# A two-layer diffusion backbone on one Trainium2 core: a third score bank, fill matmuls ordered against the scores, and modulation steps moved to other stages

## The chip, the core and the metric

The kernel runs on one NeuronCore of a Trainium2 chip, in float32 throughout. A core has five engines with instruction queues of their own: TensorE (PE in the profile, its weight loads PEld), VectorE (DVE), ScalarE (ACT), GpSimd (POOL) and SyncE (SP, which here only issues DMAs). Matmuls write to PSUM, which this program divides into 8 banks of 128 x 512 float32; all other tiles lie in SBUF. The metric is the device time of one execution in microseconds (us), the median of several runs.

## The reference

Two layers work on 1024 latent tokens (a 16 x 64 grid) and 256 context tokens, all of width 1024. In each layer every token is normalized and modulated by a shift, a scale and a gate, which come from a product of a condition vector with a 1024 x 3072 matrix (the "modulation"; the latents have one condition, the context another). Layer 0 is grouped attention (a global half A and a windowed half B), layer 1 a convolution module beside neighbourhood attention.

```python
for i in range(2):
    sh_l, sc_l, g_l = split3(silu(c)     @ mod_w[i] + mod_b[i])
    sh_c, sc_c, g_c = split3(silu(c_ctx) @ mod_w[i] + mod_b[i])
    h_lat = rms_norm(x_lat, norm_g[i]) * (1 + sc_l) + sh_l
    h_ctx = rms_norm(x_ctx, norm_g[i]) * (1 + sc_c) + sh_c
    if i == 0:
        y_lat, y_ctx = even_mixer(h_lat, h_ctx, ...)
    else:
        y_lat, _ = odd_mixer(h_lat, h_ctx, ...)     # the context is not updated
    x_lat = x_lat + g_l * y_lat
    if i == 0: x_ctx = x_ctx + g_c * y_ctx
return rms_norm(x_lat, final_g)

# even_mixer: q, k, v, gate = h @ w_in, 16 query heads on 4 key heads
#   A: RMS-normed q and k, rotary, softmax over all 1280 keys
#   B: rotary, softmax over 256 context keys and a band of +-128, with a sink logit
#   y = concat(o * silu(gate)) @ w_out
# odd_mixer: 31-tap depthwise convolution + LayerNorm on 512 channels,
#   and 8 heads that each see 8 x 16 neighbours and the context, with a bias table
```

The last layer's context is not updated, so of layer 1's gate only the latents' side is needed.

## The kernel before

The order of the work is not written out instruction by instruction. The program traces its operations in order, gives each a priority, and a planner (with a cost model of its own) then puts the instructions of each engine into one fixed order and assigns buffers. `later(n)` adds `n` to the priority number of what is traced in it, so that it gives way to other work that is ready. `tc.issue_after(x)` orders TensorE instructions of a block behind the instruction `x` on TensorE's own queue; it adds no wait on the chip beyond that order.

**Three-term products.** Each float32 operand is split into a high part (a cast on ScalarE) and a low part (a subtraction, mostly on GpSimd), `split` at L294. A product is then three matmuls, `mm3` (L317): high x high, high x low, low x high.

**Layer 0.** The four key heads are four units `u`, taken in the order 2, 3 (half B, 42 score tiles each) and 0, 1 (half A, 84 tiles each). I call them the first to the fourth pair. The stages are:

- Startup: x is loaded, shift and scale of layer 0 are computed by `mod_half` and `mod_half_v`, and h is made.
- Solo (`solo[0]` is true): `fill0(0)` (L865, L872) projects q, k, v of the first pair and half of its gate, with no attention beside it.
- Three stages of the loop at L883. `weave` (L495) steps the attention generator `attn_gen` (L392) `nmain` times and deals `nfill` steps of a second generator between: `proj_qkv` and `proj_gate` of the next pair. `NSTEP` holds a unit's steps (two a tile), `NLAST` (L50) how many of them lie beside the gate, `NFILL` (34 each) the steps of the projection of q, k and v. Fill is traced with `later(80)` (`FL`).
- The fourth pair's attention runs beside `out0_part` (L1009), the output projection of the finished pairs; `O1` (L71) deals attention steps to its four pieces. Then come the last output projection and the norm of layer 1 (L1055 to L1096).

A tile in `attn_gen` is: a score of two matmuls (L465, L469; for masked tiles one more), an exponential on ScalarE (L477, `pf`), the split into `ph` and `pl` (L479), and, three tiles later (`LOOK0`), three matmuls into the sum `ov` (L409 to L411). Before a group of 512 queries starts, `attn_prep` (L364) computes row maxima through `mx` banks (L576, L588, L596), transposes them (`trn`, L387) and writes them into QL.

**PSUM.** `BUFS` (L97) deals the 8 banks: `pp` 2 (projections), `mx` 2 (maxima), `st` 2 (scores), `ov` 1, `tr` 1. The `tr` bank holds the transposes of projected q and k (`trk`, L836), those of the maxima, the sums of modulation (`trm`, L223) and the sums of squares (`trs`, L248). In solo stages `pp` requests go round over `pp` and `mx`.

**Modulation.** `mod_steps` (L849) yields eight halves (two of layer 0's gate, then six of layer 1's shift, scale and gate, 512 columns each). A half is eight rows of weights, each one step: a load of the row (L202 or L211, on SP), and for each condition one multiply-add on VectorE (L214, L219). Outside the solo stage the second condition's rows 1, 3 and 6 go to ScalarE and GpSimd instead (L216, L217). A ninth step sums over partitions with TensorE. `tick` (L739) is called three times in each block of 24 projection matmuls and takes a modulation step at every call in the solo stage and at every third otherwise (`TICK0, TICK1`).

**Layer 1.** Four convolution projections with the convolution beside them, then `d_proj(0)` and `d_proj(1)` (L1167), the second with the LayerNorm steps of L1125 beside it, then the attention with `d_proj(2)`, `d_proj(3)` and the output projection woven in.

Of the kernel before, what the change touches and what calls it, by code (L numbers as in the profile page):

```python
# [49 lines left out]
NLAST = (48, 28)  # L50
# [18 lines left out]
NFILL = (34, 34, 34)  # L69
HV = (('gggvvvvg',) * 3, ('gggvvvvg', 'vvvgvvvg', 'gggvvvvg'))  # L70
O1 = (6, 84, 46, 14)  # L71
TICK0, TICK1 = (1, 3)
# [15 lines left out]
def tile_kernel(ctx: ExitStack, tc: tile.TileContext, a, out):  # L88
# [8 lines left out]
    BUFS = {"pp": 2, "mx": 2, "st": 2, "ov": 1, "tr": 1}  # L97
# [3 lines left out]
    sts, pvs = [], []  # L101

# [66 lines left out]
    def mod_half(pool, l, part, j):  # L169
# [11 lines left out]
        tr = bank("tr", nm("trm"))  # L181
# [11 lines left out]
    def mod_half_v(pool, l, part, j, conds):  # L193
# [28 lines left out]
        for n_, (q, t) in enumerate(zip(conds, accs)):  # L222
            tr = bank("ov" if solo[0] else "tr", nm("trm"))  # L223
# [20 lines left out]
    def rstd_steps(pool, accs, n, tag, inv=1.0, tr="tr"):  # L244
# [70 lines left out]
    done = [None]  # L315
# [48 lines left out]
    def attn_prep(pool, g):  # L364
# [21 lines left out]
        tr2 = bank("tr", nm("trn"))  # L386
# [5 lines left out]
    def attn_gen(pool, groups, vshare, look, nexts=None):  # L392
# [57 lines left out]
        for x, (g, t) in enumerate(items):  # L450
# [14 lines left out]
            sts.append(PE.matmul(st[:, :n], KA[:, cs], g.QH[:, q0 : q0 + n], start=True, stop=False))  # L465
# [29 lines left out]
    def weave(main, nmain, fill, nfill, last=True, all_fill=True, lag=0):  # L495

        done = 0
        for k in range(nmain):
            next(main, None)
            while done * nmain < (k + 1) * nfill:  # L500
                with ExitStack() as cx:
                    cx.enter_context(later(FL[layer[0]]))
                    if lag and len(sts) >= lag:
                        cx.enter_context(tc.issue_after(sts[-lag].ins))
                    next(fill, None)
                done += 1
# [145 lines left out]
    with ExitStack() as p0x:  # L652
# [6 lines left out]
        with tc.tile_pool(name="st0", bufs=1, reuse_waits="tile") as st0:  # L659
# [31 lines left out]
            def norm_bc(c, acc):  # L691
                n = CHUNKS[c][1]
                return run(rstd_steps(st0, [acc], n, "st"))[:, :n]
# [45 lines left out]
        def tick():  # L739
            beat[0] += 1  # L740
            if beat[0] % (TICK0 if solo[0] else TICK1) == 0:
# [25 lines left out]
        def proj_gate(u, ms):  # L767
# [4 lines left out]
            for m, c in ms:  # L772
                t0, n = CHUNKS[c]
                pp = bank("pp", nm("pg"))
                for dk in range(DK):
# [3 lines left out]
                    if dk % 3 == 1:  # L779
                        tick()  # L780
# [8 lines left out]
        def proj_qkv(u, w):  # L789
            wh, wl = w or load_w0("ev_qkv", u, 384)  # L790
            for jp in range(5):
                pc = ap.tile([P, 2, 384], F32, tag="pc", name=nm("pc"), bufs=PCB)
                for jj in range(2):
                    j = 2 * jp + jj
                    pp = bank("pp", nm("pq"))
                    for dk in range(DK):
                        mm3(pp[:, :384], Hs(h, 0, j * P, P, dk), Hs(h, 1, j * P, P, dk), wh[dk], wl[dk],
                            dk == 0, dk == DK - 1)
                        if dk % 3 == 1:
                            tick()  # L800
# [33 lines left out]
        def qk_tail(u, j, pc):  # L834

            tr = bank("tr", nm("trk"))  # L836
# [12 lines left out]
        def mod_steps():  # L849
# [3 lines left out]
            for part in range(3):  # L853
                for j in range(2):
                    yield from mod_half_v(ap, 1, part, j, (0, 1) if part < 2 else (0,))
# [27 lines left out]
        for k in range(3):  # L883
            u = ORDER[k]
            n = NSTEP[u // 2] + (12 if k == 0 else 0)
# [3 lines left out]
            weave(main, n - n0 - NLAST[u // 2], fill0(k + 1), NFILL[k], False)  # L889
            weave(main, NLAST[u // 2], proj_gate(ORDER[k + 1], gblocks(k + 1)[1]), 18, False)  # L890
# [79 lines left out]
    with tc.tile_pool(name="o0", bufs=1, reuse_waits="tile", side="right") as op_:  # L970
# [93 lines left out]
        weave(main, O1[1], out0_part(parts[0]), 48, False)  # L1064
        weave(main, O1[2], chain(load_oh(parts[1]), out0_part(parts[1])), 30, False)
# [568 lines left out]
```

## Time and profile before

| | us |
|---|---|
| median of 3 runs | 1557.82 |
| lowest and highest run | 1554.83, 1560.38 |
| the profiled execution | 1555.72 |
| its span (first to last instruction) | 1553.9 |
| mean granted TensorE clock | 0.967 of full speed |

Times in rows of the profile count from the span's start. "Busy" is the time in which an engine ran at least one instruction. A row of a group ends with the idle time of its engine just before its instructions and what ended most of it. The granted clock of a stretch is the mean share of full speed that TensorE had.

### The profile page before, as it was taken

The page shows a single profiled execution, that of the slowest core. Times are in us where ns is not written, and L with a number is a line of the kernel's source. Part 1 is how long each engine was busy: PE and PEld are TensorE (multiplying, and loading weights), DVE is VectorE, ACT ScalarE, POOL GpSimd, SP SyncE. Part 2 cuts the span into 40 slices and gives each one's busy share as a digit, 9 for nine tenths or more (in the row PEclk, how much of TensorE's full clock was granted, in tenths as well). Part 3 has the DMA queues.
Part 4 walks back from the last instruction along what each step waited for, and adds up shares of the span by engine and source line. Part 5 has one row for each costly group of instructions (what it writes and reads, how often), then busy time and mean ns, then how long its engine had stood idle before and what let it go on. Part 6 is the DMA issues. An engine that isn't in the chain of part 4 may idle for free.

```text
span 1553.9 us, 22052 instructions
## 1 busy us (share of the span) xinstructions
PE 1449.1 (93%) x6984; PEld 1172.3 (75%) x6984; DVE 1123.3 (72%) x2172; ACT 759.8 (49%) x1545; POOL 833.5 (54%) x762
## 2 busy tenths in 40 slices
PE   6989989999999989899999889999999999799995
PEld 1878868887789678678887668888787787687784
DVE  4998898689858666654577677999755457586776
ACT  2721354445454755565455555443434455545563
POOL 1561464555555676675455666664542443545574
PEclk9999999999999999999999999999999999899996
DMA  9548245423441124631111121213456888788623
GB/s 339 194 146 270 79 125 174 147 64 121 151 129 44 54 89 143 207 115 56 42 45 35 68 95 57 80 63 123 158 178 222 272 225 263 221 264 240 192 92 109
DMA packets 185614, 221.01 MB, mean 142 GB/s; under 512 B 17421, under 2 KB 139481, under 8 KB 185497
## 3 DMA queue, kind: packets, MB, share of 16 engines
q1 hardware_dynamic: 178832, 208.03, 43.1%
q10 hardware_dynamic: 6664, 11.57, 2.3%
q8 instruction: 55, 0.90, 0.2%
q14 instruction: 63, 0.51, 0.1%
HBM read 159.51 MB, written 60.03 MB: 141 GB/s over the span
## 4 chain that ended last, share of the span: by engine, by line
PE 67%; DVE 12%; DMA 11%; issue 3%; POOL 3%; ACT 2%; SPq 2%; DVEq 0%; ACTq 0%; POOLq 0%
PE p L320 6%; PE p L318 6%; PE p L319 6%; PE ov L409 4%; PE ov L410 4%; PE ov L411 4%; PE st L465 4%; PE po L318 4%; PE st L469 4%; PE po L319 4%; PE po L320 4%; PE pq L320 2%; PE pq L319 2%; PE pq L318 2%; DMA mw<-in_mod_w_dram 2%
## 5 line engine op out<-in xcount | busy, mean ns | idle before, releaser
L299 POOL TENSOR_TENSOR pl<-pf,ph 128x512 fp32r<-128x512 f32 (+4 forms) x321 | 399.9, 1258 | 270.7 <-ACT ph L296 218.9
L299 POOL TENSOR_TENSOR wl<-wr,wh 128x256 fp32r<-128x256 f32 (+2 forms) x256 | 197.7, 788 | 227.9 <-ACT wh L296 203.3
L477 ACT ACTIVATE pf<-st 128x512 f32<-128x512 f32 x284 | 166.2, 596 | 161.7 <-PE st L469 106.3
L296 ACT CAST ph<-pf 128x512 fp32r<-128x512 f32 (+4 forms) x364 | 209.2, 588 | 25.5 <-PE ov L410 17.6
L296 ACT CAST wh<-wr 128x256 fp32r<-128x256 f32 (+2 forms) x264 | 103.2, 404 | 172.2 <-DMA wr<-in_od_d_dram 39.3
L318 PE MATMUL p<-hh,wh 128*128 128x512 f32 x448 | 177.7, 399 | 3.7 <-DVE spk L299 1.4
L319 PE MATMUL p<-hl,wh 128*128 128x512 f32 x448 | 177.9, 398 | 0.2 <-POOL hl L299 0.2
L320 PE MATMUL p<-hh,wl 128*128 128x512 f32 x448 | 175.2, 399 | 0.1
L465 PE MATMUL st<-QH,KAt 128*128 128x512 f32 (+4 forms) x364 | 144.0, 397 | 19.8 <-ACT pf L477 16.5
L409 PE MATMUL ov<-ph,Vt 128*128 128x512 f32 (+4 forms) x364 | 143.6, 394 | 8.8 <-DVE y L631 6.4
L411 PE MATMUL ov<-pl,Vt 128*128 128x512 f32 (+4 forms) x364 | 143.7, 395 | 3.9 <-POOL pl L299 3.8
L410 PE MATMUL ov<-ph,Vt 128*64 128x512 f32 (+4 forms) x364 | 140.8, 387 | 0.0
L469 PE MATMUL st<-QL,KBt 68*128 68x512 f32 (+4 forms) x364 | 138.2, 388 | 0.8 <-DVE QL L388 0.7
L1116 DVE SCALAR_TENSOR_TENSOR cps<-U,taps,cps 128x512 f32<-128x512 f32 x184 | 124.3, 747 | 0.0
L589 DVE TENSOR_REDUCE mp<-mx 128x1 f32<-128x512 f32 x128 | 85.5, 682 | 33.5 <-PE mx L588 32.7
L219 DVE SCALAR_TENSOR_TENSOR macc<-mw,csil,macc 128x512 f32<-128x512 f32 x107 | 97.5, 929 | 14.0 <-DMA mw<-in_mod_w_dram 13.2
L318 PEld LDWEIGHTS p<-hh,wh 128*128 128x128 f32 x448 | 84.6, 189 | 24.5 <-DVE spk L299 1.6
L465 PEld LDWEIGHTS st<-QH,KAt 128*128 128x128 f32 x364 | 69.8, 192 | 42.5 <-ACT pf L477 25.3
L319 PEld LDWEIGHTS p<-hl,wh 128*128 128x128 f32 x448 | 84.6, 189 | 20.4 <-POOL hl L299 0.6
L320 PEld LDWEIGHTS p<-hh,wl 128*128 128x128 f32 x448 | 84.6, 189 | 20.3 <-POOL wl L299 1.0
L411 PEld LDWEIGHTS ov<-pl,Vt 128*128 128x128 f32 x364 | 71.1, 195 | 28.1 <-POOL pl L299 7.6
L409 PEld LDWEIGHTS ov<-ph,Vt 128*128 128x128 f32 x364 | 71.5, 196 | 24.3 <-issue 7.0
(277 smaller groups left out, 3518.4 us busy)
## 6 DMA issues: line engine op xcount, KB each, us to landing
mw<-in_mod_w_dram SPq DMA_DIRECT2D x34, 512.0 KB, 5.6
bs<-in_d_bs_dram SPq DMA_DIRECT2D x16, 832.0 KB, 7.3
Q<-qs SPq DMA_DIRECT2D x40, 256.0 KB, 2.7
QH<-Q SPq DMA_DIRECT2D x80, 128.0 KB, 2.7
bm<-in_d_bm_dram SPq DMA_DIRECT2D x16, 540.0 KB, 6.1
wr<-in_od_d_dram SPq DMA_DIRECT2D x64, 128.0 KB, 2.6
mw<-in_mod_w_dram SPq DMA_DIRECT2D x28, 256.0 KB, 3.1
wr<-in_ev_qkv_dram SPq DMA_DIRECT2D x32, 192.0 KB, 3.8
```

The lines of the kernel that those rows point to most:

```text
L296: SC.copy(hi, src)
L299: (GP if leng == "g" else VE).tensor_tensor(lo, src, hi.bitcast(F32), op=ALU.subtract)
L318: PE.matmul(o, lh, rh, start=first, stop=False)
L319: PE.matmul(o, lh, rl, start=False, stop=False)
L320: done[0] = PE.matmul(o, ll, rh, start=False, stop=last)
L409: PE.matmul(o, V[:, 64:192], ph[:, :n], start=(t == 0), stop=False)
L410: PE.matmul(g.ov[0:64, q0 : q0 + n], V[:, 0:64], ph[:, :n], start=False, stop=False)
L411: pvs.append(PE.matmul(o, V[:, 64:192], pl[:, :n], start=False, stop=(last and g.sink is None)))
L465: sts.append(PE.matmul(st[:, :n], KA[:, cs], g.QH[:, q0 : q0 + n], start=True, stop=False))
L469: PE.matmul(st[:, :n], KB[0:68, cs], g.QL[0:68, q0 : q0 + n], start=False, stop=True)
L477: SC.activation(pf[:, :n], st[:, :n], AF.Exp, scale=1.0 if g.bias else SCALE)
L1116: VE.scalar_tensor_tensor(pc, uc, w, pc, op0=ALU.mult, op1=ALU.add)
```

## The change

- PSUM: `st` gets three banks, `tr` is gone. Its users move: transposed maxima and modulation sums to `mx`, transposed q and k to `TRV`, which is `pp`, sums of squares in startup and LayerNorm to `st`.
- Attention steps: `NLAST` now goes by stage, 28, 28, 56. The third stage ends 36 steps earlier (`SHIFT`), and these steps run at the start of the next one, where `O1` becomes 6, 110, 66.
- Fill: in the first two stages of the loop a fill step may not be ordered ahead of the score eight back (`LOOSE`). In the third and in the output projections it may not be ahead of the score four back (`HOLD`), and a score may not be ahead of the last fill matmul two fill steps back (`TIE`). The third stage's first eight fill steps are traced ahead of it (`NPRE`).
- Modulation: a step at every second tick in the solo stage, at every second beside a gate and at every third beside the projection of pairs 2 and 3; none beside that of pairs 0 and 1, which also normalize q and k. Layer 1's gate leaves `mod_steps` and becomes `mod_gate1`, stepped beside `d_proj(1)`.

```diff
-NLAST = (48, 28)
+NLAST = (28, 28, 56)
+HOLD, TIE, LOOSE = 4, 2, 8
+NPRE = (0, 0, 8)
-O1 = (6, 84, 46, 14)
-TICK0, TICK1 = (1, 3)
+O1 = (6, 110, 66, 14)
+SHIFT = 36
+TICKS, TICKQ, TICKG = (2, 3, 2)
...
-    BUFS = {"pp": 2, "mx": 2, "st": 2, "ov": 1, "tr": 1}
+    BUFS = {"pp": 2, "mx": 2, "st": 3, "ov": 1}
+    tied = [None]
...
-        tr = bank("tr", nm("trm"))
+        tr = bank("st", nm("trm"))
...
-            tr = bank("ov" if solo[0] else "tr", nm("trm"))
+            tr = bank("ov" if solo[0] else "mx", nm("trm"))
...
-        tr2 = bank("tr", nm("trn"))
+        tr2 = bank("mx", nm("trn"))
...
-    done = [None]
+    done = prods = [None]
...
-            sts.append(PE.matmul(st[:, :n], KA[:, cs], g.QH[:, q0 : q0 + n], start=True, stop=False))
+            with ExitStack() as cx:
+                if tied[0] is not None:
+                    cx.enter_context(tc.issue_after(tied[0].ins))
+                sts.append(PE.matmul(st[:, :n], KA[:, cs], g.QH[:, q0 : q0 + n], start=True, stop=False))
...
-    def weave(main, nmain, fill, nfill, last=True, all_fill=True, lag=0):
+    def weave(main, nmain, fill, nfill, last=True, all_fill=True, lag=0, tie=0):
         done = 0
+        past = []
         for k in range(nmain):
+            tied[0] = past[-tie] if tie and len(past) >= tie else None
             next(main, None)
+            tied[0] = None
             while done * nmain < (k + 1) * nfill:
...
                     next(fill, None)
+                past.append(prods[0])
                 done += 1
...
-        def tick():
+        def tick(every):
             beat[0] += 1
-            if beat[0] % (TICK0 if solo[0] else TICK1) == 0:
+            if beat[0] % (TICKS if solo[0] else every) == 0:
...
-                        tick()
+                        tick(TICKG)
...
-                            tick()
+                            if u > 1:
+                                tick(TICKQ)
...
-            tr = bank("tr", nm("trk"))
+            tr = bank(TRV, nm("trk"))
...
-            for part in range(3):
+            for part in range(2):
                 for j in range(2):
-                    yield from mod_half_v(ap, 1, part, j, (0, 1) if part < 2 else (0,))
+                    yield from mod_half_v(ap, 1, part, j, (0, 1))
...
-            n = NSTEP[u // 2] + (12 if k == 0 else 0)
+            n = NSTEP[u // 2] + (12, 0, -SHIFT)[k]
...
-            weave(main, n - n0 - NLAST[u // 2], fill0(k + 1), NFILL[k], False)
-            weave(main, NLAST[u // 2], proj_gate(ORDER[k + 1], gblocks(k + 1)[1]), 18, False)
+            hold = dict(lag=HOLD, tie=TIE) if k == 2 else dict(lag=LOOSE)
+            fill = fill0(k + 1)
+            for _ in range(NPRE[k]):
+                with later(FL[0]):
+                    next(fill)
+            weave(main, n - n0 - NLAST[k], fill, NFILL[k] - NPRE[k], False, **hold)
+            weave(main, NLAST[k], proj_gate(ORDER[k + 1], gblocks(k + 1)[1]), 18, False, **hold)
...
-        weave(main, O1[1], out0_part(parts[0]), 48, False)
-        weave(main, O1[2], chain(load_oh(parts[1]), out0_part(parts[1])), 30, False)
+        weave(main, O1[1], out0_part(parts[0]), 48, False, lag=HOLD, tie=TIE)
+        weave(main, O1[2], chain(load_oh(parts[1]), out0_part(parts[1])), 30, False, lag=HOLD, tie=TIE)
...
-        nh = [norm_h(0, "st", "tr"), norm_h(1, "pp", "tr"), norm_h(2, "st", "tr")]
-        weave(main, NSTEP[U1 // 2] - O1[0] - O1[1] - O1[2], through_attention(), O1[3])
+        nh = [norm_h(0, "st", "mx"), norm_h(1, "pp", "mx"), norm_h(2, "st", "mx")]
+        weave(main, NSTEP[U1 // 2] + SHIFT - O1[0] - O1[1] - O1[2], through_attention(), O1[3])
...
+    def mod_gate1():
+
+        for j in range(2):
+            c0 = 2048 + j * 512
+            acc = kvp.tile([P, 512], F32, tag="QH", name=nm("macc"), bufs=3)
+            for dk in range(DK):
+                w = kvp.tile([P, 512], F32, tag="QL", name=nm("mw"), bufs=3)
+                SY.dma_start(w, a["mod_w"][1, dk * P : (dk + 1) * P, c0 : c0 + 512])
+                if dk == 0:
+                    VE.tensor_scalar(acc, w, csil[:, dk, 0:1], None, op0=ALU.mult)
+                else:
+                    VE.scalar_tensor_tensor(acc, w, csil[:, dk, 0:1], acc, op0=ALU.mult, op1=ALU.add)
+                yield
+            tr = bank("ov", nm("trm"))
+            for i in range(4):
+                PE.matmul(tr[:, 2 * i : 2 * i + 2], acc[:, i * P : (i + 1) * P], one, start=True, stop=True)
+            o = 16 + j * 4
+            VE.tensor_tensor(modT[1][:, o : o + 4, 0], tr[:, 0:8].rearrange("p (i c) -> p i c", c=2)[:, :, 0],
+                             modb[:, 1, o : o + 4], op=ALU.add)
+            yield
...
-            bc = yield from rstd_steps(vp, [s1], 512, "st", 2.0)
+            bc = yield from rstd_steps(vp, [s1], 512, "st", 2.0, "st")
...
             bg = lns()
+            m1 = mod_gate1()
             for _ in d_proj(1):
                 pump(1)
+                next(m1, None)
             for _ in bg:
                 pass
+            run(m1)
```

More of the change, by code (lines that the diff above doesn't have):

```diff
@@ L242, in newton_rsqrt, with rstd_steps @@
         return r
-    def rstd_steps(pool, accs, n, tag, inv=1.0, tr="tr"):
+    def rstd_steps(pool, accs, n, tag, inv=1.0, tr="mx"):
         nb = n // P
@@ L692, in norm_bc @@
                 n = CHUNKS[c][1]
-                return run(rstd_steps(st0, [acc], n, "st"))[:, :n]
+                return run(rstd_steps(st0, [acc], n, "st", tr="st"))[:, :n]
             made = [0]
```

## The prediction

> **What bounds the kernel now.** I read the page first, then busy time by stage, then who waits inside the stages that the change touches.
>
> ```profile
> span 1553.9 us, 22052 instructions
> PE 1449.1 (93%) x6984; PEld 1172.3 (75%) x6984; DVE 1123.3 (72%) x2172; ACT 759.8 (49%) x1545; POOL 833.5 (54%) x762
> ```
>
> TensorE is busy for 93% of the span, so 104.8 us of it are idle. The same number of matmuls runs after the change, so a gain can only come out of idle or slow TensorE time. The stages (columns: length, then busy us and instructions of PE, PEld, DVE, ACT, POOL, then granted clock, DMA share, GB/s):
>
> ```profile
> 60.00:160.00 100.00, 92.48 (x527) 85.67 (x526) 91.64 (x131) 32.48 (x68) 42.44 (x34) 0.97 0.58 182
> 160.00:290.00 130.00, 123.91 (x632) 103.69 (x632) 103.83 (x228) 59.75 (x139) 68.82 (x57) 0.96 0.42 126
> 290.00:460.00 170.00, 160.40 (x821) 134.28 (x820) 138.01 (x294) 83.89 (x184) 93.86 (x77) 0.99 0.40 121
> 460.00:660.00 200.00, 186.49 (x871) 147.98 (x870) 137.86 (x249) 111.80 (x200) 131.32 (x100) 0.97 0.34 106
> 660.00:880.00 220.00, 219.13 (x1038) 174.84 (x1037) 138.47 (x248) 119.95 (x227) 131.57 (x113) 1.00 0.20 64
> 880.00:920.00 40.00, 29.48 (x128) 22.45 (x127) 28.25 (x49) 24.46 (x53) 26.15 (x27) 0.83 0.07 20
> 1120.00:1210.00 90.00, 87.78 (x430) 71.77 (x429) 42.94 (x83) 33.09 (x72) 32.24 (x35) 1.00 0.63 203
> ```
>
> In order these are the solo stage (first pair's projections beside modulation), the attention of the first, second and third head pair with the next pair's projections as fill, the fourth pair with the output projection, layer 0's end, and layer 1's second pair of projections. Stage 660 to 880 is full: 0.9 us idle at clock 1.00. The five others of layer 0 idle for 7.5, 6.1, 9.6, 13.5 and 10.5 us. Idle time also costs clock:
>
> ```profile
> 404.50:406.50 2.00, 0.06 (x2) 0.08 (x1) 1.93 (x3) 1.89 (x4) 1.88 (x2) 1.00 0.58 171
> 406.50:409.90 3.40, 3.40 (x12) 2.80 (x13) 3.40 (x6) 0.00 (x0) 1.88 (x2) 0.50 0.26 86
> 563.50:570.30 6.80, 6.16 (x15) 4.38 (x15) 2.06 (x5) 3.90 (x8) 4.50 (x7) 0.50 0.27 80
> ```
>
> A pause of 2 us at 404.5 is followed by 3.4 us at half clock, which is 1.7 us more lost. Taken as length times (1 - clock), the five stages lose 3.0, 5.2, 1.7, 6.0 and 6.8 us that way. So 10.5, 11.3, 11.3, 19.5 and 17.3 us are to be had, 69.9 us in all. The Trainium skill, TensorE: Matmul & The Clock Gate, "HAM oscillation — how this bites in real kernels", says that pauses longer than about 3.4 us bring the low clock. By it the 2 us pause would cost only itself, and the low clock would have another cause that stays; the rows show it right behind 2 us, which is shorter. What that would make of the sum is a rival below.
>
> What ends the idle time (waits of TensorE, us in total, times, longest), first for 60 to 160, then 160 to 460, then 460 to 660, then 880 to 920:
>
> ```profile
> PE trk L838 <- DVE qs L299: 6.3, 4, 2.8
> ```
> ```profile
> PE st L465 <- ACT pf L477: 6.3, 8, 2.1
> PE mx L596 <- DVE mp L578: 2.6, 3, 1.4
> PE mx L576 <- DMA QH<-Q: 1.9, 1, 1.9
> ```
> ```profile
> PE st L465 <- ACT pf L477: 7.4, 6, 2.3
> PE mx L576 <- DMA QH<-Q: 2.0, 3, 0.8
> ```
> ```profile
> PE ov L409 <- DVE y L631: 5.1, 1, 5.1
> ```
>
> In the solo stage the one `tr` bank waits for a VectorE that is 92% busy. In the attention stages a score waits for one of two `st` banks, while no fill matmul stands before it in the queue.
>
> **The change, part by part.**
>
> *Modulation moved off the solo stage.* These groups stand in 60 to 160, 160 to 290 and 290 to 450:
>
> ```profile
> L219 DVE SCALAR_TENSOR_TENSOR macc<-mw,csil,macc 128x512 f32<-128x512 f32 x61 | 52.4, 879 | 3.0 <-DMA mw<-in_mod_w_dram 2.3
> L214 DVE TENSOR_SCALAR macc<-mw,csil 128x512 f32<-128x512 f32 x10 | 7.4, 751 | 0.0
> ```
> ```profile
> L219 DVE SCALAR_TENSOR_TENSOR macc<-mw,csil,macc 128x512 f32<-128x512 f32 x18 | 20.3, 1138 | 4.3 <-DMA mw<-in_mod_w_dram 4.2
> ```
> ```profile
> L219 DVE SCALAR_TENSOR_TENSOR macc<-mw,csil,macc 128x512 f32<-128x512 f32 x14 | 14.2, 1015 | 6.8 <-DMA mw<-in_mod_w_dram 6.7
> ```
>
> The solo stage has 39 ticks (30 of the projection, 9 of the gate). Each now gives a step; after, every second does. With the step that completes a loaded pair of weight rows that is 40 steps now, 36 of them rows with two operations each, and 20 after, 18 of them rows. The last step's second operation runs on ScalarE and GpSimd, so VectorE has 71 now (61 + 10 above) and 35 after. 36 operations at 0.88 us leave it: 31.7 us of its 91.6. Then TensorE decides: in back-to-back runs a 384-wide matmul starts every 0.175 us and a 512-wide one every 0.234 us (first and last of each run):
>
> ```profile
> 553.33 0.34 PE L319 MATMUL pq<-wl,hh 128*128 128x384 f32 x1
> 553.86 0.34 PE L319 MATMUL pq<-wl,hh 128*128 128x384 f32 x1
> ```
> ```profile
> 959.68 0.39 PE L318 MATMUL p<-hh,wh 128*128 128x512 f32 x1
> 961.55 0.40 PE L318 MATMUL p<-hh,wh 128*128 128x512 f32 x1
> ```
>
> That puts the stage's TensorE work at 87 us, an estimate: roughly 275 of 384 columns (48), 96 of 512 (22.5), 48 of 256 (5.6), and about 11 for sums and transposes. 13 us are open by this count, 10.5 by the rows; I take **-10**, bounds -20 (the modelled ends of matmuls hide more idle time) and 0.
>
> *The same modulation in attention.* The steps left for it hold 12 two-sided rows and 16 one-sided ones now; after, 30 two-sided rows (the one-sided go to layer 1). With ScalarE and GpSimd doing rows 1, 3 and 6 of the second side, VectorE goes from 36 to 49 operations: 13 more, 14 us at 1.08 us (the mean of the two rows 1138 and 1015), most of it in 160 to 290 (23 of the 34 steps: 4 at the gate left over, 10 beside the plain projection, 9 at its gate). None falls on the projections of the third and fourth pair, where VectorE also normalizes. ScalarE and GpSimd get 12 such operations in place of 5, at 0.72 and 1.28 us each:
>
> ```profile
> L216 ACT ACTIVATE mw<-mw,csil x5: 722/722/727, 158.2 to 242.5; 128x512 f32<-128x512 f32 x5
> L217 POOL TENSOR_TENSOR macc<-macc,mw x5: 1276/1287/1293, 163.4 to 245.1; 128x512 f32<-128x512 f32 x5
> ```
>
> VectorE is 80% busy in 160 to 290, so the 14 us fit into its 26 idle ones only if they come evenly; that is what bounds this term below.
>
> *Third score bank, fill bound loosely (160 to 460).* With three banks a score may start while two wait for ScalarE. Fill may no longer run more than eight scores ahead, so it is there when scores wait. Against it stand the moved steps. Of 22.6 us I take half, **-11**, bounds -22 and +8 (the 14 us, half hidden).
>
> *Where the `tr` bank's users go.* Transposes of q and k share two `pp` banks with the projections. Each holds its bank for a cast and a subtraction, and 40 of them bound the cost at 41 us with no cover:
>
> ```profile
> L296 ACT CAST qs<-trk x40: 460/478/492, 77.3 to 639.4; 128x384 fp32r<-128x384 f32 x40
> L299 DVE TENSOR_TENSOR qs<-trk,qs x40: 510/554/559, 87.3 to 639.9; 128x384 fp32r<-128x384 f32 x40
> ```
> ```profile
> L388 DVE TENSOR_TENSOR QL<-trn,k_bd x56: 681/682/684, 178.2 to 1490.8; 4x512 fp32r<-4x512 f32 x36, 12x512 fp32r<-12x512 f32 x20
> ```
>
> Cover is the attention beside them; without it each costs about 1 us. The transposed maxima share `mx` and hold it 0.68 us, 56 times, 38 us uncovered; they run whole tiles before their scores. Both at 0.
>
> *Third pair: fewer attention steps, fill tied to scores, eight fill steps ahead (460 to 660).* 36 steps, 18 tiles, move on to the fourth pair's stage, so 60 tiles beside 34 fills become 38 beside 26. The move itself is neutral: five matmuls a tile cost the same in either stage. It also pulls the fourth pair's start past this boundary, where output weights and k land:
>
> ```profile
> 640.00:655.00 15.00, 11.92 (x42) 7.58 (x40) 11.90 (x23) 8.20 (x13) 11.33 (x8) 0.89 0.91 287
> ```
> ```profile
> PE po L318 <- ACT wh L296: 1.1, 1, 1.1
> ```
>
> That boundary alone loses 3.1 us idle and 1.6 of clock. Of 19.5 us I take two thirds, **-13**, bounds -19 and 0.
>
> *Fourth pair and layer 0's end.* Output projections spread over 182 of 204 steps in place of 136 of 168, so 14 fills meet the last 22 steps, not 32. The stage is full, so more evenness gives nothing there; a stall of the tie is a rival below. At the end, 5.1 us go by until the group before has been divided and leaves the only `ov` bank, with no fill to run. I take **-4**, bounds -12 and +6.
>
> *Layer 1.* 16 operations of one side come to 1120 to 1210, and 16 loads of 256 KB on SP's queue. Uncontended the operation takes 0.75 us:
>
> ```profile
> L219 DVE SCALAR_TENSOR_TENSOR macc<-mw,csil,macc x107: 734/751/2014, 15.3 to 447.1; 128x512 f32<-128x512 f32 x107
> ```
> ```profile
> L1163 DVE SCALAR_TENSOR_TENSOR uc<-uc,gc 128x512 f32<-128x512 f32 x8 | 5.5, 687 | 9.1 <-DMA gc<-Gc 9.1
> ```
>
> That is 12 us on a VectorE with 47 idle; 4.2 MB at 203 / 0.63 = 322 GB/s is 13 us, with 33 free. But a step that waits for its load holds the LayerNorm behind it, which waits 9.1 us for its own loads and ends just before layer 1's attention can start. I take **+3**, bounds 0 and +12. Layer 1's attention gets the third bank and loses `tr`: **-1**, bounds -4 and +4. The startup uses `st` for sums: 0.
>
> Sum: -10 - 11 - 13 - 4 + 3 - 1 = **-36**. The profiled execution took 1555.72 us (1.8 beside its span), so 1519.7; the median of the runs is 2.1 higher, so **1522**.
>
> **The rivals.**
>
> *VectorE becomes the bound in 160 to 460.* For: 80 to 81% busy, single operations stretched to 1.1 us there, 14 us more. Against: steps go beside gates. The stage's term becomes +4 and half of solo's gain is lost: -16, **1542**.
>
> *The tie stalls attention (slower).* A score now stands behind a fill matmul two fills back in TensorE's queue; when that waits for weights, everything waits. The chain per weight set is load, cast, subtraction:
>
> ```profile
> wr<-in_ev_wo_dram SPq DMA_DIRECT2D x32, 128.0 KB, 2.2
> ```
> ```profile
> L296 ACT CAST wh<-wr 128x256 fp32r<-128x256 f32 (+2 forms) x264 | 103.2, 404 | 172.2 <-DMA wr<-in_od_d_dram 39.3
> L299 POOL TENSOR_TENSOR wl<-wr,wh 128x256 fp32r<-128x256 f32 (+2 forms) x256 | 197.7, 788 | 227.9 <-ACT wh L296 203.3
> ```
>
> That is 3.4 us, with half clock 5.1. Ten sets pass in the tied stages: +51, so +15 net, **1573**; it turns slower from the eighth stalled set. Against: 660 to 880 loads eight of these sets today and idles 0.9 us.
>
> *It does not do what it says.* The planner already places fill so that neither bound binds, and VectorE's work only changes place: solo -10, +7 in attention, +3 in layer 1: about **1558**.
>
> *The low clock does not follow the pauses,* so only idle time can be won: of the terms -38 in layer 0 a share of 22.7 / 69.9, 12 us, falls away: -24, **1534**.
>
> *All of it is recovered:* the longer lookahead and the tie leave no pause to 920: -69.9 + 3 - 1 = -68, **1490**.
>
> **How the numbers follow.** Forecast (1500 to 1545) 0.50; VectorE bound 0.14; tie stalls 0.16; no effect 0.09; clock apart 0.05; all recovered 0.06. The range 1490 to 1573 takes in all of these up to their prices, hence every bound that I hold likely; what it leaves out are several bad ends together. Measurement cannot tell 0.3%, 4.7 us, from no change. Faster: 0.50 + 0.14 + 0.05 + 0.06 = 0.75; same 0.09; slower 0.16.
>
> **What would show it.** Right: the solo stage's VectorE near 60 us and its length near 90; score waits for `pf` well under 13.7 us up to 660; half-clock stretches gone from 160 to 660; clock 1.00 over the third pair; the last wait for `y` shorter. Wrong: TensorE waits of `p`, `po` or `pg` for `wh` or `wl` (tie), `mx` waits for `mp` grown (VectorE), `pq` waits for `qs` or `pc` (shared bank), first `mx` of layer 1 late against the last `uc` (modulation there).

## The result, and the profile after

The changed kernel takes **1641.08 us** (median of 4 runs, 1637.82 to 1642.6) against 1558.13 us for the kernel before (4 runs on the same chip): a ratio of 1.0531, 95% interval [1.0505, 1.0558]. I had forecast 1522 us with a range up to 1573. The direction was wrong, and so was the range. The profiled execution took 1637.82 us, 82.1 more than the one of before.

The page after, total, engines and granted clock:

```profile
span 1635.9 us, 22000 instructions
PE 1489.7 (91%) x6984; PEld 1200.6 (73%) x6984; DVE 1138.8 (70%) x2165; ACT 766.4 (47%) x1552; POOL 842.9 (52%) x769
PEclk9999989899999989999999988999999999899996
```

The same 6984 matmuls run, but TensorE now idles for 146.2 us of the span, not 104.8, and its mean clock fell from 0.967 to 0.941. Where the time lies is read off marks that both traces have, each the first start of a group (us from the span's start):

| mark | before | after | stage longer by |
|---|---|---|---|
| first maximum (attention starts) | 158.9 | 126.4 | -32.5 |
| first maximum of the third pair | 457.6 | 511.2 | +86.1 |
| first output projection of layer 0 | 652.6 | 701.2 | -5.1 |
| first projection of layer 1 | 923.6 | 980.0 | +7.7 |
| first convolution step | 960.5 | 1029.3 | +12.5 |
| first maximum of layer 1 | 1212.7 | 1287.8 | +6.3 |
| end | 1553.9 | 1635.9 | +6.9 |

The first two rows belong together, since the solo stage only handed its work on: +53.6 us by the third pair's first maximum. Layer 1 adds 25.7. The third pair's stage is 5.1 shorter, but fewer matmuls fall in it (see e8). By stage (columns as in the prediction's stage table):

```profile
60.00:125.00 65.00, 58.24 (x328) 53.34 (x327) 58.73 (x80) 27.10 (x58) 38.38 (x29) 0.95 0.44 138
125.00:290.00 165.00, 141.14 (x691) 119.93 (x691) 98.25 (x208) 58.08 (x131) 63.36 (x54) 0.91 0.38 118
290.00:512.00 222.00, 201.52 (x967) 167.66 (x968) 168.21 (x345) 98.16 (x215) 119.05 (x94) 0.94 0.35 104
512.00:702.00 190.00, 175.14 (x805) 140.68 (x804) 129.53 (x229) 104.18 (x189) 121.92 (x92) 0.95 0.31 95
```

From 125 to 512 TensorE idles for 23.9 + 20.5 = 44.4 us, and length times (1 - clock) is 14.9 + 13.3 = 28.2 us: 72.6 together. The two rows of before from 160 to 460 had 15.7 + 6.9 = 22.6. The 50 us between them are nearly all of the 53.6. VectorE is only 60% and 76% busy there, so it isn't short of time. TensorE's waits over the whole span say what is missing:

```profile
PE trn L391 <- DVE nmt L387: 18.6, 8, 5.2
...
PE st L476 <- DVE QL L392: 9.0, 7, 2.6
PE st L472 <- ACT pf L484: 8.4, 12, 3.1
PE mx L587 <- DVE QL L392: 7.9, 9, 2.3
PE pq L322 <- ACT pc L814: 6.8, 2, 4.4
...
PE pq L322 <- DVE sg L344: 4.1, 3, 3.0
```

Score waits for `pf` did fall to 8.4 us; before had

```profile
PE st L465 <- ACT pf L477: 16.5, 17, 2.3
```

What took their place is the end of a group's preparation: `trn` waits for `nmt`, the VectorE result that it transposes, and scores and maxima wait for QL. The eight waits of `trn` shown all lie in 125 to 512. In 160 to 460 of before, `trn` waited twice, for 0.6 and 0.5 us. The third kind of new wait is `pq` for `pc` and `sg`: a projection wants a `pp` bank that another user has not yet emptied.

### The profile page after: what moved, and what is told of

Its sections match the earlier page's. It is cut to its first block, busy times and chain, and to the rows that moved or that the text cites. A ratio compares the mean times of both kernels' runs of the same rounds, so it can differ in the third digit from the quotient of the medians.

```text
span 1635.9 us, 22000 instructions
## 1 busy us (share of the span) xinstructions
PE 1489.7 (91%) x6984; PEld 1200.6 (73%) x6984; DVE 1138.8 (70%) x2165; ACT 766.4 (47%) x1552; POOL 842.9 (52%) x769
## 4 chain that ended last, share of the span: by engine, by line
PE 68%; DMA 12%; DVE 11%; issue 3%; POOL 2%; ACT 2%; SPq 1%; ACTq 0%; DVEq 0%; POOLq 0%
PE p L322 6%; PE p L324 6%; PE p L323 6%; PE st L476 4%; PE st L472 4%; PE ov L413 4%; PE ov L414 4%; PE ov L415 4%; PE po L322 4%; PE po L323 4%; PE po L324 3%; DMA mw<-in_mod_w_dram 3%; PE pq L322 3%; PE pq L324 3%; PE pq L323 3%
## 5 line engine op out<-in xcount | busy, mean ns | idle before, releaser
L300 ACT CAST ph<-pf 128x512 fp32r<-128x512 f32 (+4 forms) x364 | 209.0, 588 | 27.0 <-PE ov L414 14.9
L322 PE MATMUL p<-hh,wh 128*128 128x512 f32 x448 | 181.7, 407 | 11.4 <-ACT hh L300 6.0
L472 PE MATMUL st<-QH,KAt 128*128 128x512 f32 (+4 forms) x364 | 147.7, 408 | 11.0 <-ACT pf L484 8.4
L322 PEld LDWEIGHTS p<-hh,wh 128*128 128x128 f32 x448 | 86.1, 192 | 34.3 <-ACT hh L300 6.1
L223 DVE SCALAR_TENSOR_TENSOR macc<-mw,csil,macc 128x512 f32<-128x512 f32 x86 | 82.2, 981 | 29.7 <-DMA mw<-in_mod_w_dram 29.1
L322 PE MATMUL pq<-wh,hh 128*128 128x384 f32 x256 | 90.6, 354 | 6.8 <-ACT pc L814 6.8
L324 PE MATMUL pq<-wh,hl 128*128 128x384 f32 x256 | 89.5, 351 | 1.1 <-DVE hl L314 0.7
```

What stands on the lines that cost most here:

```text
L300: SC.copy(hi, src)
L322: PE.matmul(o, lh, rh, start=first, stop=False)
L324: done[0] = PE.matmul(o, ll, rh, start=False, stop=last)
```

## The experiments

"Before + x" means that x alone was put into the kernel before; "after - x" that x alone was undone. All ratios are to the kernel before on the same chip (its medians there 1557 to 1559 us).

| run | kernel | us | ratio [95%] |
|---|---|---|---|
| e1_banks | before + all PSUM edits | 1615.12 | 1.0381 [1.0338, 1.0424] |
| e2_old_banks | after - all PSUM edits | 1575.85 | 1.0107 [1.0075, 1.0139] |
| e4_deal | before + the deal of steps | 1575.91 | 1.0119 [1.0082, 1.0156] |
| e5_mods | before + modulation | 1589.14 | 1.0169 [1.0133, 1.0204] |
| e3_trn_mx | before + `trn` in `mx` | 1590.66 | 1.0195 [1.015, 1.024] |
| e9_trn_st | after, `trn` in `st` | 1619.04 | 1.0398 [1.0377, 1.0419] |
| e12_trk_pp_only | before + `trk` in `pp` | 1577.85 | 1.0137 [1.0119, 1.0155] |
| e6_trk_pp | e1, but `tr` kept for `trn`, `st` 2 | 1580.02 | 1.0133 [1.0091, 1.0175] |
| e7_two_st | e1 with `st` 2 | 1607.18 | 1.0297 [1.0272, 1.0323] |
| e8_no_loose | e4 without LOOSE | 1555.84 | 0.9987 [0.9965, 1.001] |
| e14_after_no_loose | after - LOOSE | 1633.26 | 1.0483 [1.0445, 1.0521] |
| e15_old_banks_no_loose | e2 without LOOSE | 1585.85 | 1.0178 [1.0141, 1.0214] |
| e10_gate_held | e5, gate's loads held in place | 1591.22 | 1.0223 [1.0202, 1.0244] |
| e13_solo_rate | e10, every tick in the solo stage | 1589.38 | 1.0193 [1.0153, 1.0233] |
| e11_deal_gate | e8 + held gate alone | 1562.61 | 1.003 [1.0008, 1.0052] |
| e16_fill60 | before, another fill priority | 1561.75 | 1.0018 [0.9992, 1.0044] |
| e17_late60 | before, another step priority | 1567.4 | 1.004 [1.0014, 1.0065] |
| e18_tick4 | before, a step each fourth tick | 1565.21 | 1.0039 [1.0012, 1.0066] |

### Which part costs the time: e1, e2, e4, e5

e1 and e2 take all lines of the PSUM part of the diff, e4 all of `NLAST`, `SHIFT`, `O1`, `NPRE`, `LOOSE`, `HOLD` and `TIE`, e5 all of the ticks and `mod_gate1`.

> The kernel before with the PSUM part of the change alone: st gets a third bank, the tr bank is gone and its users go to mx, pp and st. Theory A (the transposed maxima in mx put each group's transposition ahead of the next group's maxima in the same ring, and the chain of preparation becomes longer): most of the loss is here, 1600 to 1650 us, TensorE waits of trn for nmt of 10 us or more. Rival B (fill and scores bound to each other cost the time): 1545 to 1565 us. Rival C (modulation moved into attention makes VectorE late): 1545 to 1565 us.

> The changed kernel with the PSUM part undone (st 2, tr 1, every user back in tr); the deal of fill, the binding and the moved modulation stay. Theory A: the loss goes, 1520 to 1560 us, the wait of trn for nmt under 3 us. Rival B: 1620 to 1645 us. Rival C: 1600 to 1645 us.

> The kernel before with the deal of fill alone: NLAST, SHIFT, O1, NPRE, the lags of 8 and 4 and the tie of 2; banks and modulation as before. Theory A: 1535 to 1560 us. Rival B: 1600 to 1640 us, with waits of fill matmuls for their weights. Rival C: 1535 to 1560 us.

> The kernel before with the modulation part alone: a step at every second tick in the solo stage, at every second beside gates, at every third beside plain projections, none beside the third and fourth pair's; layer 1's gate beside its second projection. Theory M1 (layer 0 gains about 20 us, as between the runs with the deal alone and with deal and modulation, and layer 1 gives about 8 back): 1540 to 1552 us. Rival M2 (the 13 further operations make VectorE late in the first two attention stages): 1563 to 1580 us.

Alone, the parts cost 56, 17 and 30 us; taken out of the whole, PSUM is worth 65. So PSUM is the largest, but no part wins anything. The sum, 103, is more than the 82.95 measured, and deal and modulation together (e2, 17) cost less than modulation alone: the parts don't add up, and each price holds for its surroundings. e1 came out as theory A has it, with 9.5 us of `trn` waiting for `nmt` where I had put 10 or more. The three others missed: e2 stayed above theory A's 1560, e4 fell between its ranges, and e5, at 30 us, lies above even M2.

### The transposed maxima: e3, e9

```diff
 # e3, on before
-        tr2 = bank("tr", nm("trn"))
+        tr2 = bank("mx", nm("trn"))
 # e9, on after
-        tr2 = bank("mx", nm("trn"))
+        tr2 = bank("st", nm("trn"))
```

> The kernel before with one line changed: the transposed maxima (trn) take an mx bank; tr stays for all other users, st stays at 2. Theory A: slower by 20 to 80 us (1578 to 1640), and in the trace the next maximum follows trn at once in TensorE's order. Rivals B and C, and a variant of A in which the third score bank or the shared pp banks do it: 1550 to 1565 us.

> The changed kernel with one line mended: the transposed maxima (trn) take a bank of st, of which there are three, in place of one of mx. Theory A (the maxima's own ring is what delays the next group): in the trace maxima no longer follow trn at once, and 20 to 40 us of the 83 come back, 1600 to 1620 us. Rival A3 (any shared ring is as bad, since trn then holds scores back): 1630 to 1660 us.

**One word costs 32 us**; moved out of `mx`, `trn` gives 22 of the whole kernel's time back, though it then takes its place among the scores. e9 is still 43 us above e2, so the other PSUM moves cost as well. Now the mechanism. TensorE around one transpose (start, duration, instruction, idle time before it), before:

```profile
197.56 0.37 PE L387 MATMUL trn<-ident,nmt 128*12 128x128 f32 x1 [0.60 <-DVE nmt L377]
197.59 0.78 PE L465 MATMUL st<-QH,KAt 128*128 128x512 f32 x1
198.30 0.79 PE L409 MATMUL ov<-ph,Vt 128*128 128x512 f32 x1
```

In e3:

```profile
230.47 0.46 PE L320 MATMUL pg<-hc,wl 128*128 128x256 f32 x2
230.78 0.27 PE L387 MATMUL trn<-ident,nmt 128*12 128x128 f32 x1
230.80 0.48 PE L576 MATMUL mx<-KAt,QH 128*128 128x256 f32 x2
```

And after:

```profile
240.52 0.38 PE L391 MATMUL trn<-ident,nmt 128*12 128x128 f32 x1 [5.16 <-DVE nmt L387]
240.62 0.77 PE L587 MATMUL mx<-KAt,QH 128*128 128x256 f32 x2
241.68 1.22 PE L476 MATMUL st<-QL,KBt 68*128 68x512 f32 x2 [0.29 <-DVE QL L392]
```

In e3 and after, a maximum of the *next* group follows right behind `trn`. Counted in TensorE's matmuls up to 520 us, the median distance from `trn` to the next maximum is 1 in after, e1 and e3, but 8 in before, 11 in e2, 6.5 in e12 and 12 in e9, where `trn` has left that ring. Banks of one tag are handed out in the order in which the program asks, and the next group's maxima ask after `trn`. With `trn` in their ring they can't be planned ahead of it, and `trn` stands at the end of a chain through VectorE. The planner answers by pushing `trn` back (a median of 30 to 35 matmuls behind the last maximum, against 13 in before), or TensorE stands still as at 235. Either way a group's preparation no longer overlaps that of the next, and the scores run out: 137 score matmuls run from 160 to 450 in e3, 175 in before. The unbound fill of e3 simply runs ahead of the starved attention:

```profile
L588 PE MATMUL mx<-KAt,QH x128: 388/396/628, 547.5 to 902.1; 128*128 128x512 f32 x128
```
```profile
160.00:300.00 140.00, 52.43 (x263) 45.31 (x261) 5.17 (x11) 0.96 0.44 134
300.00:450.00 150.00, 62.73 (x309) 54.39 (x309) 6.23 (x13) 0.99 0.37 111
```

The second fence is busy time of `pq` alone in e3, in two stages; before had 212 and 226 matmuls there. In e3 the output projections start at 534.2 us, before the third pair has its first maximum at 547.5 (before: 652.6 and 457.6). What is left of the attention then has no cover.

### The other banks: e12, e6, e7

```diff
 # e12, on before
-            tr = bank("tr", nm("trk"))
+            tr = bank(TRV, nm("trk"))
 # e6, on e1
-    BUFS = {"pp": 2, "mx": 2, "st": 3, "ov": 1}
+    BUFS = {"pp": 2, "mx": 2, "st": 2, "ov": 1, "tr": 1}
-        tr2 = bank("mx", nm("trn"))
+        tr2 = bank("tr", nm("trn"))
 # e7, on e1
-    BUFS = {"pp": 2, "mx": 2, "st": 3, "ov": 1}
+    BUFS = {"pp": 2, "mx": 2, "st": 2, "ov": 1}
```

> The kernel before with one line changed: the transposes of q and k take a pp bank. Theory P1 (sharing pp with the projections is what e6 loses): 1572 to 1585 us. Rival P2 (e6 loses by the modulation sums in mx or the sums of squares in st): 1553 to 1565 us.

> The kernel before with all PSUM moves but two: the transposed maxima keep the tr bank for themselves, and st stays at 2. So q and k transposes are in pp, the modulation sums in mx, the sums of squares in mx and st. Theory A1 (the moved maxima are the larger part of the loss, the other users the 24 us between e3 and e1): 1575 to 1590 us. Rival A2 (only the maxima's ring matters, and the 24 us come from their meeting the third bank): 1553 to 1566 us.

> The PSUM part alone, as in e1, but with two score banks, so one of the eight banks stays unused. Theory S1 (the third score bank wins time where a score waited for pf): 1622 to 1640 us, slower than e1. Rival S2 (it wins nothing, since the chain of preparation is what attention waits for): 1608 to 1622 us, as e1.

`trk` in `pp` costs 20 us by itself (e12), which is nearly all of e6's 21, where the modulation sums and the sums of squares move as well. From 60 to 960 us of e12, `trk` waits 5.4 us for `pc` and `pq` 2.7 us, which before has neither of: transposes and projections now queue for the same two banks. That places 8 of the 20 us at most; the rest isn't placed. And the third score bank, the one edit meant to gain, **gained nothing**: with an eighth bank left unused e7 is 8 us faster than e1, a difference that another order alone can make (e16 to e18). The score wait it was to remove is there in e7 and smaller in e1:

```profile
PE st L465 <- ACT pf L477: 11.0, 13, 2.3
```
```profile
PE st L465 <- ACT pf L477: 4.4, 6, 1.3
```

So the bank does remove 6.6 us of waits by name, and the time isn't shorter: TensorE waits elsewhere. The Trainium skill, Perfetto Trace Analysis, "Matmul Optimizations", asks that all 8 PSUM banks be used; here the eighth, in e1 against e7, won nothing. Step by step, each against the kernel before on its own chip, e12, e6, e7 and e1 add 21, 0, 27 and 8 us, which are the 56 of e1.

### The deal of steps: e8, e14, e15

```diff
-            hold = dict(lag=HOLD, tie=TIE) if k == 2 else dict(lag=LOOSE)
+            hold = dict(lag=HOLD, tie=TIE) if k == 2 else {}
```

> The deal of fill alone, as in e4, but without the lag of eight scores in the first two stages. Theory D1 (the loose bound costs the 12 us that e4 loses before the third pair's maxima): 1555 to 1567 us. Rival D2 (the loss comes from the tie, or from the changed places of the steps): 1570 to 1580 us.

> The changed kernel without the lag of eight scores in the first two stages; all else as changed. Theory L1 (the bound takes away the fill that covered slow preparation, 20 us as between e4 and e8): 1612 to 1628 us. Rival L2 (with the slow ring of maxima and modulation beside it, the bound keeps fill for later and pays): 1640 to 1665 us.

> Deal and modulation with the old banks, as e2, without the lag of eight scores. If the parts add up (modulation +28, deal without the lag -2): 1578 to 1592 us. If the lag costs 20 us here as well: 1550 to 1562 us. If it is neutral beside the moved modulation: 1570 to 1580 us.

On the deal alone, LOOSE is worth the whole loss: 1575.91 with it, 1555.84 without. Fill matmuls of the projection (`pq`), then of the gate (`pg`), in e4:

```profile
160.00:300.00 140.00, 35.82 (x174) 31.27 (x172) 3.65 (x8) 0.91 0.37 113
...
160.00:300.00 140.00, 25.71 (x113) 19.81 (x114) 2.20 (x4) 1.94 (x4) 0.91 0.37 113
```

and in e8:

```profile
160.00:300.00 140.00, 41.11 (x209) 36.42 (x209) 4.12 (x9) 0.96 0.43 130
...
160.00:300.00 140.00, 32.55 (x144) 24.29 (x144) 3.57 (x6) 3.14 (x6) 0.96 0.43 130
```

With 78 score matmuls run in that stage in e4 and 79 in e8, the lag holds back 66 fill matmuls and wins no score; the clock falls from 0.96 to 0.91. My reading, which no run tests by itself, is that in the first pair the attention is slow because its preparation is, and fill running ahead was its cover. But the effect doesn't carry over: LOOSE costs 8 us in the changed kernel (e14) and *helps* by 10 with the old banks and the new modulation (e15). Both are hardly more than order alone moves, so what it does beside the modulation isn't settled.

e8 is the deal as I had meant it. Its third pair, first maximum to first output projection, takes 187.2 us (before 195.1, after 190.0). But fewer matmuls fall in it. Before, e8 and after:

```profile
457.00:652.00 195.00, 184.39 (x864) 146.87 (x862) 137.04 (x250) 111.26 (x200) 129.94 (x99) 0.97 0.32 98
```
```profile
459.00:646.00 187.00, 177.60 (x838) 142.79 (x836) 130.55 (x236) 106.61 (x194) 124.25 (x94) 0.97 0.33 99
```
```profile
511.00:701.00 190.00, 175.09 (x803) 140.29 (x802) 129.53 (x228) 104.51 (x189) 120.92 (x91) 0.95 0.31 94
```

Idle time and length times (1 - clock) come to 16.5 us in before, 15.0 in e8 and 24.4 in after. So the stage is shorter because 26 and 61 matmuls run elsewhere, and hardly because it waits less; in after it waits more. The fourth pair takes 272.0 us in e8 (before 271.0) with 24 more matmuls, and idles for 7.2 us where before idles for 13.7. The tie did not stall it: from 459 to 920 one output projection waits for weights, 2.2 us, and in the changed kernel none from 511 to 983. As a whole, e8 is 0.9987 of before, and its interval takes in 1.

### Modulation: e10, e13, e11

```diff
 # e10, on e5
-                SY.dma_start(w, a["mod_w"][1, dk * P : (dk + 1) * P, c0 : c0 + 512])
+                with tc.issue_after(raws[-1].ins):
+                    SY.dma_start(w, a["mod_w"][1, dk * P : (dk + 1) * P, c0 : c0 + 512])
 # e13, on e10
-TICKS, TICKQ, TICKG = (2, 3, 2)
+TICKS, TICKQ, TICKG = (1, 3, 2)
 # e11, on e8: mod_gate1 held as in e10, ticks as in before
```

> The modulation part alone, as in e5, with the loads of layer 1's gate ordered behind the weight loads of layer 1's second projection on SP's queue, so that the planner can't pull them ahead to the layers' boundary. Theory G1 (the pulled steps delay layer 1's norm on VectorE by 10 us): 1576 to 1582 us, and the stretch from the first p matmul to the first cps operation is 37 us as before, not 46.6. Rival G2 (the boundary is longer for another reason): 1586 to 1592 us.

> As e10 (the modulation part alone, layer 1's gate held in its place), but with a modulation step at every tick of the solo stage, as before; 14 two-sided steps are left for attention. Theory R1 (the 20 steps that leave the solo stage win nothing there and cost about 20 us in attention): 1560 to 1573 us, the layer 1 part still 12 us longer. Rival R2 (where steps lie in attention, beside gates, is what costs): 1580 to 1592 us.

> What the runs so far let stand together: banks as before, the deal of fill without the lag of eight, layer 1's gate beside its second projection with its loads held there as in e10, and the old rates of modulation steps (every tick in the solo stage, every third otherwise). If the 16 one-sided operations cost time in layer 0 and not in layer 1: 1540 to 1553 us, under e8. Rival: they were hidden before, 1553 to 1562 us.

**The gate of layer 1** didn't stay where it was written. Its 16 loads (`mw` in after, then in e10):

```profile
L1123 SPq DMA_DIRECT2D mw<-in_mod_w_dram x16: 327/328/394, 987.6 to 1007.2; - x16
```
```profile
L1108 SPq DMA_DIRECT2D mw<-in_mod_w_dram x16: 327/370/537, 1133.1 to 1169.4; - x16
```

Nothing but priority bound them to `d_proj(1)`, and the planner pulled them up to the boundary between the layers, onto VectorE, in front of layer 1's norm of x:

```profile
1002.69 0.76 DVE L1127 SCALAR_TENSOR_TENSOR macc<-mw,csil,macc 128x512 f32<-128x512 f32 x1 [1.10 <-DMA mw<-in_mod_w_dram]
1004.04 1.54 DVE L1127 SCALAR_TENSOR_TENSOR macc<-mw,csil,macc 128x512 f32<-128x512 f32 x2 [0.60 <-DMA mw<-in_mod_w_dram]
1006.38 0.75 DVE L1127 SCALAR_TENSOR_TENSOR macc<-mw,csil,macc 128x512 f32<-128x512 f32 x1 [0.80 <-DMA mw<-in_mod_w_dram]
1007.72 0.75 DVE L1127 SCALAR_TENSOR_TENSOR macc<-mw,csil,macc 128x512 f32<-128x512 f32 x1 [0.59 <-DMA mw<-in_mod_w_dram]
...
1009.65 4.03 DVE L310 SCALAR_TENSOR_TENSOR x<-x,gs,bc 128x512 f32<-128x512 f32 x6
```

Ordering the loads behind the weights of `d_proj(1)` (e10) brings that boundary back to 36.8 us (before 36.9, e5 46.6). It wins nothing: the stretch from the first convolution step to the first maximum of layer 1 goes from 252.2 to 264.0. It is no idle time. In e10, then in before:

```profile
975.00:1240.00 265.00, 258.01 (x1193) 208.98 (x1192) 205.50 (x335) 107.11 (x206) 132.58 (x131) 1.00 0.48 153
```
```profile
960.00:1213.00 253.00, 248.65 (x1145) 201.32 (x1144) 190.79 (x313) 104.85 (x200) 130.99 (x131) 1.00 0.43 139
```

48 more matmuls run ahead of that first maximum: it comes late, as the LayerNorm behind the gate's steps does (its last step ends 255.7 us after the first convolution step, before 243.2), and projections are done in its place. They then lack as cover later: from the first maximum to the end it takes 348.4 us, against 341.2. From layer 1's first projection to the end the gate costs 17 to 20 us in e5, e10 and e13 (647.2, 649.2, 650.5, before 630.3), 14 in e11 (644.5). In e11, where these steps are gone from layer 0, that layer ends 6.0 us earlier than in e8, no more than order alone moves; the whole is 7 us slower than e8.

**The solo stage.** VectorE was relieved as meant, and the attention starts 34.5 us earlier in e5 (124.4). The work isn't done earlier. All of it from 60 to 200, in before and in e5:

```profile
60.00:200.00 140.00, 129.44 (x720) 117.71 (x719) 126.09 (x204) 47.77 (x105) 62.63 (x50) 0.96 0.48 148
```
```profile
60.00:200.00 140.00, 128.58 (x694) 117.22 (x693) 109.26 (x186) 53.45 (x116) 68.21 (x55) 0.95 0.39 121
```

17 us of VectorE are gone, TensorE does no more. Among what it now waits for are the first keys, which the early attention needs:

```profile
124.39 0.74 PE L576 MATMUL mx<-KAt,QH 128*128 128x256 f32 x4 [2.65 <-DMA KAt<-K]
```

e13 gives the solo stage its old rate of steps and keeps the rest; its attention starts at 165.2 and it takes as long as e10. So in sum the moved solo steps are worth nothing either way.

**Layer 0 in all** starts layer 1 at 942.6 (e5), 938.5 (e10) and 939.7 (e13) in place of 923.6: 15 to 19 us later. That loss I can place only in part. In e5 and e10, 460 to 640 has 8.0 and 7.3 us of waits of `mx` for `mp` (before 2.1), a VectorE late with maxima; in e13, where the last two-sided step starts at 243 us (478 in e10), the loss lies before 250 (200 to 250: TensorE 39.2 us busy, before 47.0). It goes where the two-sided steps go, which speaks for them, but no run without them and with all else alike was made.

### How much order alone moves: e16, e17, e18

```diff
 # e16: FL = (60, -98) in place of (80, -98)    e17: LATE = 60 in place of 100
 # e18: TICK0, TICK1 = (1, 4) in place of (1, 3)
```

> The kernel before with the fill's priority number at 60 in place of 80: the same instructions, another order from the planner. Theory N1 (any new order costs 15 to 30 us here, so that the parts that cost as much in e5, e6, e12 and e13 show no mechanism of their own): 1573 to 1590 us. Rival N2 (orders of the same work differ by a few us only, and the parts' losses are theirs): 1553 to 1566 us.

> The kernel before with the modulation's priority number at 60 in place of 100: the same instructions, another order from the planner. N1: 1573 to 1590 us; N2: 1553 to 1566 us.

> The kernel before with a modulation step in attention at every fourth tick in place of every third: the same work, spread further. N1: 1573 to 1590 us; N2: 1553 to 1566 us.

Changes that only give the planner another order cost 4 to 9 us, as N2 has it (e17 is 1 us above its range). Three orders are few, but the costs of 20, 30 and 32 us above lie well beyond them; the 3 to 10 us by which e8, e11, e14, e15 and e7 differ from their neighbours are of their size.

## Why the prediction was wrong

**The step that failed is "Where the `tr` bank's users go ... Both at 0".** It had the right places: 38 us uncovered for the maxima, 41 for q and k. Measured alone are 32 and 20. That 38 lies near 32 is luck, since it sums up holding times, those of layer 1 too. Two errors stand behind the zero. I priced how long a user *holds* a bank (0.68 us) and not whom it stands *in front of*: the next group's maxima, behind a chain through VectorE. "They run whole tiles before their scores" is true of before because `tr` was a ring of its own; the change takes that away. And the bounds that I had written out never reached the range: +79 us would have made it end near 1600, and 1641 would still have lain outside.

**Third score bank and lag, -11.** Score waits fell as forecast, from 6.3 us in 160 to 460 to these in 125 to 512 after:

```profile
PE st L472 <- ACT pf L484: 1.1, 3, 0.5
```

Their time didn't come back: +8 for the bank (e1 against e7), and for LOOSE +20 on the deal alone (e4 against e8), far outside the bound of +8, and +8 in the changed kernel (e14). I had read unbound fill as waste that runs away; on the deal alone, holding it back won no score.

**Solo stage, -10.** VectorE's 58.7 busy us lie near my 60 by luck: I meant 60 of about 90 us, and the stage ended after 66 with VectorE 90% busy. The gain was 0. A stage's length isn't its work: matmuls that no longer lie before the first maximum lie behind it. And a next wait, for keys that come by DMA, was not named.

**Third pair, -13.** The stage is 7.9 shorter in e8 and 5.1 after, but not as I meant it: idle and slow time, which the term was taken from, fell by 1.5 us in e8 and grew by 7.9 in after. The rest is matmuls that run elsewhere. **Fourth pair and end, -4.** It held in e8: the wait for `y` falls from 5.1 to 0.8 us and idle time by 6.5, though with more matmuls the stage is 1.0 longer. In after the wait for `y` is gone too, but between 640 and 960 scores wait 5.4 us for QL and `ov` 4.3 for `ph`, and the stage is 7.7 longer.

**Layer 1's gate, +3, bounds 0 and +12.** Measured +14 to +20. I had the mechanism (a step in front of the LayerNorm) and took the place from the program's text. The planner chose another; held in its place it cost as much.

**Modulation in attention**, which I had inside the bounds of another term at most +8, cost 15 to 19 us of layer 0, cause only partly shown.

**The rivals.** VectorE as the bound (1542) is wrong as put: it is less busy in these stages than before. The tie (1573), my slower case, didn't happen: no wait for weights. So the kernel got slower by a mechanism that I had written down as a bound and as a sign ("`pq` waits for `qs` or `pc`, shared bank") but never as a rival; for `trn`, the larger part, not even a sign was named. That half clock would be gone up to 660 was wrong too: 0.91 to 0.95 there.

**Still open**: where most of the 20 us of `trk` goes, what the two-sided modulation steps do to layer 0, whether LOOSE really helps beside them, as it hurts without, and why layer 1's attention is 2 to 7 us longer in most variants. No version tried beats the kernel before beyond its interval.

## What to carry to other kernels

A buffer ring doesn't only lend space, it orders its users: before putting the end of one chain into the ring where the next chain begins, look in the trace at what runs between the two, for a wait on a shared bank can't be seen while the banks are separate. A bound that is written down belongs in the range, above all where its cover is said to be what the same change touches. And work with no dependency stays where it is written only if something orders it there; a wait that is removed by name is no gain until the stage is shorter.

## What the runs showed of the hardware

Short pauses cost clock, too. In e5 two waits for keys, 2.65 us before 124.39 and 1.93 us before 132.56, are each followed by a stretch at about half clock:

```profile
122.00:125.00 3.00, 0.61 (x5) 0.61 (x6) 1.71 (x2) 1.26 (x3) 2.46 (x3) 1.00 0.71 233
125.00:129.00 4.00, 4.00 (x25) 4.00 (x23) 1.52 (x5) 1.38 (x3) 1.07 (x2) 0.57 0.59 189
129.50:132.00 2.50, 1.13 (x9) 0.93 (x8) 2.50 (x6) 0.69 (x1) 0.00 (x0) 1.00 0.50 141
132.00:136.00 4.00, 3.44 (x10) 2.94 (x11) 0.20 (x1) 0.41 (x2) 2.42 (x2) 0.57 0.89 266
```

4.0 us at 0.57 is 3.4 at half clock, the same 3.4 us as behind the 2 us pause in the prediction. The Trainium skill, TensorE: Matmul & The Clock Gate, "HAM oscillation — how this bites in real kernels", warns of idle gaps above about 3.4 us; here pauses of 1.9 to 2.7 us were enough. Not every such pause does it: behind one of 2.92 us before 345.07 in e5 the clock stayed at 1.00 for 3.6 us, up to the next pause. In after, all 23 pauses of 1.9 us and more lie at such a stretch or less than 3.5 us ahead of one. This fits the 28.2 us of clock lost from 125 to 512 beside 44.4 us of idle time: a serial chain with short holes pays for them twice.
